# Head norms with tokens on the partitions: where the sums of squares of seven heads are taken

## The chip, the cores and the metric

The kernel runs on one core of one Trainium2 chip. The metric is device time in microseconds. The time before is 871.75 us, the median of three runs (871.43 to 872.48).

## The reference, cut to what matters

The program is one layer of a hybrid encoder over 512 tokens of width 1024. Two of its three branches end each head with an RMS norm over the head's 128 channels: four heads of a gated recurrence and four heads of differential attention.

```python
def rms_norm(x, g):
    xf = x.astype(jnp.float32)
    y = xf * lax.rsqrt(jnp.mean(xf * xf, axis=-1, keepdims=True) + NORM_EPS)
    return (y * g).astype(x.dtype)

# diff_attention: a = softmax(s0) - lam * softmax(s1), per head and block of 128 queries
    o = o.swapaxes(0, 1).reshape(B, S, ATT_HEADS, ATT_V_DIM)
    o = rms_norm(o, gain) * (1.0 - lambda_init)

# hgrn2_mixer: a forward and a backward scan, per head
    o = rms_norm((o_f + o_b).astype(q.dtype), gain).reshape(B, S, REC_WIDTH)
    return o * jax.nn.silu(g)
```

The kernel divides the attention weights by the first softmax's sum only after the product with the values. With Z that sum, the head's unnormalised output u stands for o = u / Z, and the norm becomes u * r with r = (1/Z) * (mean(u^2) * (1/Z)^2 + eps)^(-1/2). In the code 1/Z is `rr`, then `r0`.

## The kernel before, in words

Activations are kept transposed: channels on the 128 partitions, the 512 tokens along the free axis, in four blocks of 128 tokens (`NB`). Projections are products of a high and a low part of both operands, three terms of eight matmuls with 512 columns each, written to the PSUM tiles `mm`. Weights arrive by DMA in `raw`, and ScalarE (`whi`) and VectorE (`wlo`) split them.

The program order on TensorE is fixed when the program is built. A small planner, `Pipe.run`, holds several Python generators: one for each head and one for the stream of projection jobs. It keeps a clock `pipe.t` that each matmul and transpose advances. A generator yields `("w", t, slack)`, which means that it need not come back before t us later (and may be put off by slack), or `("e", name, t)`, which makes it wait for a mark. When no head is due, the stream issues products, in steps of two. So a head's small pieces sit between products, and the numbers in the yields decide how many products lie between. The other engines' order is made by a scheduler that simulates the program.

The recurrence head (`rec_scan`) ends with four groups of matmuls into a PSUM tile `rc`: the values `v_rec` as stationary operand against the scores `pt`, plus the states `st` against the gated queries `kq`, all 128x128 f32. The result has channels on the partitions. The attention head (`att_head`) multiplies the values (`va`) with the transposed probabilities (`aT`) into `rc`, also with channels on the partitions.

Both then call `head_norm`. ScalarE squares the tile into `sqo` and copies it into `og`, times the per-channel gain. TensorE multiplies each 128x128 block of `sqo` with a column of 1/128, which gives the mean square of 128 tokens on 128 partitions, one column of `tp` per block; with f32 operands each such matmul shows as two in the trace. VectorE adds eps (`ms`; in attention it multiplies by `r0` twice as well, `mo`), POOL takes the power -1/2 (`rso`), and in attention VectorE multiplies by `r0` again. TensorE then transposes each column of `rso`, broadcast to 128 columns, so that r lies along the free axis on all partitions. VectorE multiplies `og` with it (in the recurrence after it has multiplied with the gate `sg`), and the result is split in `y_arena` or `y_hi` and `y_lo`.

In the trace, line 96 is the helper that records matmuls and line 104 the one that records transposes. `hT` is the projection's activation, `s` a tile of exponentials, `co` the softmax coefficient that POOL computes from `zz`.

Of the kernel before, what the change touches and what calls it, by code (L numbers as in the profile page):

```python
# [11 lines left out]
F32 = mybir.dt.float32  # L12
F32R = mybir.dt.float32r
U8 = mybir.dt.uint8
AF = mybir.ActivationFunctionType
ALU = mybir.AluOpType
PSUM = bass.MemoryType.PSUM

P = 128
S = 512  # L20
D = 1024
NB = S // P
KT = D // P
HEADS = 4
FFN = 2816
FT = FFN // P
EPS = 1e-6
# [55 lines left out]
def encoder_kernel(ctx: ExitStack, tc: tile.TileContext, x, norm1_g, w_in, pool_w, pool_scale,  # L83
# [3 lines left out]
    nc = tc.nc  # L87
# [7 lines left out]
    def mm(out_, lhsT, rhs, start, stop, chain=False):  # L95
        i = nc.tensor.matmul(out_, lhsT=lhsT, rhs=rhs, start=start, stop=stop, skip_group_check=chain)  # L96
        tc.keep_in_program_order(i)
        n = 1
        for d in rhs.shape[1:]:
            n *= d  # L100
        pipe.t += max(0.107, n * 0.0004167 + 0.002) if rhs.dtype == F32R else max(0.216, n * 0.001667 + 0.004)

    def transpose(out_, in_, idn):
        tc.keep_in_program_order(nc.tensor.transpose(out_, in_, idn))  # L104
        pipe.t += 0.108
# [11 lines left out]
    small = ctx.enter_context(pool("small", 5))  # L117
    psum = ctx.enter_context(pool("psum", 3, space=PSUM))

    def bank(name, shape=(P, 512)):  # L120
        return psum.tile(list(shape), F32, name=name, bufs=2 if name == "tp" else 3)
# [7 lines left out]
    ident = const.tile([P, P], F32, name="ident")  # L129
    make_identity(nc, ident)  # L130
    fixed = const.tile([P, 2], F32, name="fixed")
    onesD, minus1 = fixed[:, 0:1], fixed[:, 1:2]
    nc.vector.memset(onesD, 1.0 / P)
    nc.vector.memset(minus1, -1.0)
    mhalf = const.tile([P, 8], F32, name="mhalf")
    nc.vector.memset(mhalf, -0.5)
# [2 lines left out]
    gain_a = const.tile([P, 1], F32, name="gain_a")  # L139
# [4 lines left out]
    gain_r = vcol[:, 13:14]  # L144

    def pow_mhalf(dst, src):
        return nc.gpsimd.tensor_tensor(out=dst, in0=src, in1=mhalf[:, :src.shape[1]], op=ALU.pow).ins  # L147

    def rsqrt_eps(dst, mean):

        ms = small.tile([P, 8], F32, name="ms")[:, :mean.shape[1]]
        eng = nc.vector if mean.space == PSUM else nc.gpsimd
        eng.tensor_scalar(out=ms, in0=mean, scalar1=1.0, scalar2=EPS, op0=ALU.mult, op1=ALU.add)  # L153
        return pow_mhalf(dst, ms)

    LAST, FF = {}, {}
# [434 lines left out]
    ps = bank("mm")  # L591
# [13 lines left out]
    ps = bank("mm")  # L605
# [17 lines left out]
    last = first_split((on_act, on_dve))  # L623
    for h, b, where in ((h0, 0, ("tp", "tp")), (h1, 1, ("rc", "mm"))):
        for half in range(2):
            with behind(last):
                on_act = rows_T(h, hT, b, half, None, where[half])
            last = on_act, LAST["hT_lo"]
# [4 lines left out]
    last = on_act, on_dve  # L633
    h2, on_dve, on_act = norm_rows(xt[2], g_b, xw, last)
    h3, on_dve, on_act = norm_rows(xt[3], g_b, xw, (on_act, on_dve))
    last = first_split((on_act, on_dve))
# [52 lines left out]
        nc.vector.tensor_copy(out=masks, in_=maskf)  # L689
    st0.close()  # L690

    def head_norm(o_ps, tmp, gain, r0=None, bufs=2, slack=0.0):


        og = tmp.tile([P, S], F32, name="og", bufs=bufs)
        sq = tmp.tile([P, S], F32, name="sqo", bufs=bufs)
        nc.scalar.activation(out=sq, in_=o_ps, func=AF.Square)
        nc.scalar.activation(out=og, in_=o_ps, func=AF.Copy, scale=gain)
        yield ("w", 1.3, slack)
        sp = bank("tp")  # L700
        for b in range(NB):
            mm(sp[:, b:b + 1], sq[:, b * P:(b + 1) * P], onesD, True, True)
        r = small.tile([P, NB], F32, name="rso")
        if r0 is None:
            rsqrt_eps(r, sp[:, 0:NB])
        else:
            m = small.tile([P, NB], F32, name="mo")
            nc.vector.tensor_tensor(out=m, in0=sp[:, 0:NB], in1=r0, op=ALU.mult)
            nc.vector.tensor_tensor(out=m, in0=m, in1=r0, op=ALU.mult)
            nc.vector.tensor_scalar(out=m, in0=m, scalar1=EPS, scalar2=None, op0=ALU.add)  # L710
            pow_mhalf(r, m)
            nc.vector.tensor_tensor(out=r, in0=r, in1=r0, op=ALU.mult)
        yield ("w", 3.55, slack)
        rb = bank("tp")
        for b in range(NB):
            transpose(rb[:, b * P:(b + 1) * P], r[:, b:b + 1].to_broadcast([P, P]), ident)
        return og, rb
# [124 lines left out]
    fronts, sgs = {}, {}  # L842
# [70 lines left out]
    def rec_scan(h):  # L913
# [85 lines left out]
                nc.vector.scalar_tensor_tensor(out=own, in0=st[:, 3 * d + prev, :], scalar=total, in1=ps[:, j, :],  # L999
                                               op0=ALU.mult, op1=ALU.add)  # L1000
        yield ("w", 2.4 if h < 3 else 1.6, slack)
        ps = bank("rc")
        for b in range(NB):
            o = ps[:, b * P:(b + 1) * P]
            mm(o, vs[b], pt[:, b, :], True, False)
            for d in range(2):
                if 0 <= b - 1 + 2 * d < NB:
                    j = b - 1 if d == 0 else b
                    mm(o, st[:, 3 * d + j, :], kq[:, 1 - d, b * P:(b + 1) * P], False, b == (0 if d else 3) or d == 1)
        mark(f"O{h}")  # L1010
        og, rbp = yield from head_norm(ps, rt, gain_r, slack=slack)
        yield ("e", f"G{h}", 0.0)
        nc.vector.tensor_tensor(out=og, in0=og, in1=sgs.pop(h), op=ALU.mult)
        nc.vector.tensor_tensor(out=og, in0=og, in1=rbp, op=ALU.mult)
        nc.scalar.copy(out=y_rec[0][:, h, :], in_=og)
        nc.vector.tensor_tensor(out=y_rec[1][:, h, :], in0=og, in1=y_rec[0][:, h, :].bitcast(F32), op=ALU.subtract)

# [72 lines left out]
    def att_head(h):  # L1090
# [64 lines left out]
                mm(ps, a[:, k, es], r[:, k, :], i == 0 and k == 0, i == 2 and k == NB - 1)  # L1155
            yield
        mark(f"PV{h}")
        og, rbp = yield from head_norm(ps, at, gain_a, rr, 1, 6.0 if h < HEADS - 1 else 0.0)
        mark(f"AN{h}")
        nc.vector.tensor_tensor(out=og, in0=og, in1=rbp, op=ALU.mult)  # L1160
        nc.scalar.copy(out=y_attn[0][:, h, :], in_=og)
        nc.vector.tensor_tensor(out=y_attn[1][:, h, :], in0=og, in1=y_attn[0][:, h, :].bitcast(F32),
                                op=ALU.subtract)
# [733 lines left out]
```

## Time and profile before

| | before |
|---|---|
| median of three runs | 871.75 us (871.43 to 872.48) |
| profiled execution, its own time | 871.81 us |
| its span | 870.0 us |
| granted TensorE clock | 0.999 |
| busy: TensorE, VectorE, ScalarE, POOL | 862.4, 659.2, 448.7, 37.1 us |
| sums of squares by matmul (`tp<-fixed,sqo`) | 64 matmul records, from 124.5 to 331.7 us |
| broadcast transposes (`tp<-ident,rso`) | 32, from 130.0 to 334.5 us |

Times in views are microseconds from the start of the span, and the duration of one instruction is in nanoseconds where a group's mean is shown. The busy time of a group of matmuls is the union of their overlapping spans, so the distance from one start to the next is a better measure of what an instruction takes from TensorE.

### The profile page before, as it was taken

To read this page: it belongs to the slowest core of one execution; us is meant where nothing else is said; L and a number is where in the kernel's file an instruction comes from. 1 tells how busy PE (TensorE), PEld (TensorE's weight loads), DVE (VectorE), ACT (ScalarE), POOL (GpSimd) and SP (SyncE) were. 2 spreads that over 40 slices of the span, in tenths; PEclk is the share of its full clock that TensorE was granted. 3 is DMA by queue.
4 is the path that set the end of the run, shared out by engine and by line. 5 is a ranking of instruction groups with operands and counts; after the bars stand their busy time and mean duration, and the time that the engine had idled before them with its cause. 6 is when DMAs were issued, how large, how long until landed. Compare 5 with 4: busy or idle time off the path is not lost.

```text
span 870.0 us, 14113 instructions
## 1 busy us (share of the span) xinstructions
PE 862.4 (99%) x5713; PEld 786.1 (90%) x5713; DVE 659.2 (76%) x979; ACT 448.7 (52%) x721; POOL 37.1 (4%) x83
## 2 busy tenths in 40 slices
PE   9999999999999999999999999999999999999997
PEld 8989998888988888899999998999999999988886
DVE  6779644845757888987776756988888888847996
ACT  6644343435757664563354425655555655533563
POOL 2000000000102220000000001000000000000001
PEclk9999999999999999999999999999999999999999
DMA  8330113024133321343332840344433433355002
GB/s 245 98 122 25 50 49 121 25 74 151 43 95 90 90 68 49 97 146 98 97 98 97 288 124 1 85 112 128 114 98 108 136 98 99 121 194 192 2 1 98
DMA packets 115694, 87.54 MB, mean 101 GB/s; under 512 B 3862, under 2 KB 104748, under 8 KB 115628
## 3 DMA queue, kind: packets, MB, share of 16 engines
q1 hardware_dynamic: 115036, 85.57, 32.2%
q8 instruction: 45, 0.74, 0.4%
q10 hardware_dynamic: 592, 1.05, 0.3%
q14 instruction: 21, 0.17, 0.1%
HBM read 84.52 MB, written 2.10 MB: 100 GB/s over the span
## 4 chain that ended last, share of the span: by engine, by line
PE 98%; issue 1%; DMA 0%; DVE 0%; POOL 0%; ACT 0%; POOLq 0%
PE mm L96 65%; PE rc L96 28%; PE tp L96 3%; PE tp L104 2%; DMA xin<-in_x_dram 0%; PE rc L104 0%; DVE hrow L502 0%; POOL rstd L147 0%; ACT silu L1479 0%; ACT x L1503 0%; DVE x L1472 0%; DVE x L1481 0%; PE mm L104 0%; POOLq L1892 0%; POOL ms L153 0%
## 5 line engine op out<-in xcount | busy, mean ns | idle before, releaser
L191 ACT CAST whi<-raw 128x1024 fp32r<-128x1024 f32 (+1 forms) x134 | 127.5, 959 | 140.7 <-PE mm L96 95.2
L192 DVE TENSOR_TENSOR wlo<-raw,whi 128x1024 fp32r<-128x1024 f32 (+1 forms) x134 | 147.8, 1106 | 50.9 <-ACT whi L191 41.3
L96 PE MATMUL mm<-hT_hi,whi 128*128 128x512 f32 (+1 forms) x344 | 81.3, 370 | 0.0
L96 PE MATMUL mm<-hT_hi,wlo 128*128 128x512 f32 (+1 forms) x344 | 80.0, 368 | 0.0
L96 PE MATMUL mm<-hT_lo,whi 128*128 128x512 f32 (+1 forms) x344 | 78.8, 367 | 0.0
L96 PEld LDWEIGHTS mm<-hT_hi,whi 128*128 128x128 f32 x344 | 59.2, 188 | 10.3 <-ACT hT_hi L515 0.2
L96 PEld LDWEIGHTS mm<-hT_lo,whi 128*128 128x128 f32 x344 | 59.1, 188 | 9.8
L96 PEld LDWEIGHTS mm<-hT_hi,wlo 128*128 128x128 f32 x344 | 58.8, 188 | 9.5
L318 DVE TENSOR_TENSOR slo<-sums,shi 128x1024 fp32r<-128x1024 f32 x54 | 65.7, 1217 | 0.0
L316 ACT CAST shi<-sums 128x1024 fp32r<-128x1024 f32 x54 | 56.8, 1052 | 4.1 <-DVE sums L280 3.3
L276 DVE TENSOR_TENSOR sums<-raw 128x1024 f32<-128x1024 f32 x27 | 32.9, 1218 | 1.2 <-DMA raw<-in_w_in_dram 1.2
L96 PE MATMUL mm<-y_arena,whi 128*128 128x512 f32 x128 | 32.7, 394 | 0.0
L96 PE MATMUL mm<-whi,y_arena 128*128 128x256 f32 (+1 forms) x192 | 32.1, 317 | 0.0
L96 PE MATMUL rc<-kq,kc 128*128 128x128 f32 x224 | 30.4, 284 | 0.0
L96 PEld LDWEIGHTS rc<-kq,kc 128*128 128x128 f32 x224 | 29.2, 191 | 1.1
L961 DVE TENSOR_TENSOR kq<-kq,pyr 128x256 f32<-128x256 f32 x48 | 18.2, 420 | 15.8 <-PE rc L96 15.8
L96 PEld LDWEIGHTS mm<-whi,y_arena 128*128 128x128 f32 x192 | 27.9, 189 | 2.6
L929 ACT COPY kc<-kq 128x512 f32<-128x512 f32 x28 | 18.6, 667 | 21.6 <-DVE kq L955 8.2
L1114 ACT ACTIVATE s<-s,mx 128x512 f32<-128x512 f32 x32 | 23.0, 719 | 10.9 <-DVE mx L1112 10.2
L96 PEld LDWEIGHTS mm<-y_arena,whi 128*128 128x128 f32 x128 | 23.7, 188 | 5.1
L1413 DVE TENSOR_TENSOR g<-mm,g 128x256 f32<-128x256 f32 x21 | 8.9, 424 | 23.9 <-PE mm L96 23.4
L96 PE MATMUL mm<-fhi,shi 128*128 128x256 f32 x168 | 25.9, 276 | 0.0
(409 smaller groups left out, 2053.5 us busy)
## 6 DMA issues: line engine op xcount, KB each, us to landing
raw<-in_w_in_dram SPq DMA_DIRECT2D x44, 512.0 KB, 4.2
raw<-in_w_ffn_in_dram SPq DMA_DIRECT2D x44, 512.0 KB, 4.1
raw<-in_w_in_dram SPq DMA_DIRECT2D x8, 1024.0 KB, 5.2
raw<-in_w_ffn_out_dram SPq DMA_DIRECT2D x7, 1024.0 KB, 4.8
raw<-in_w_out_dram SPq DMA_DIRECT2D x4, 1024.0 KB, 10.1
xin<-in_x_dram SPq DMA_DIRECT2D x4, 512.0 KB, 4.6
raw<-in_w_up_rec_dram SPq DMA_DIRECT2D x2, 1024.0 KB, 7.6
raw<-in_w_up_pool_dram SPq DMA_DIRECT2D x2, 1024.0 KB, 5.0
```

The lines of the kernel that those rows point to most:

```text
L96: i = nc.tensor.matmul(out_, lhsT=lhsT, rhs=rhs, start=start, stop=stop, skip_group_check=chain)
L104: tc.keep_in_program_order(nc.tensor.transpose(out_, in_, idn))
L191: LAST["whi"] = nc.scalar.copy(out=hi, in_=view).ins
L192: LAST["wlo"] = nc.vector.tensor_tensor(out=lo, in0=view, in1=hi.bitcast(F32), op=ALU.subtract).ins
L276: nc.vector.tensor_tensor(out=strided(sums, 0, [[2 * half, 2], [1, half]]), in0=strided(self.raw, 0, [[3 * half, 2], [1, half]]), in1=stri ...
L316: nc.scalar.copy(out=hi, in_=view)
L318: on_dve = nc.vector.tensor_tensor(out=lo, in0=view, in1=hi.bitcast(F32), op=ALU.subtract).ins
L929: nc.scalar.copy(out=strided(kc, 0, [[2 * n, S // (2 * n)], [n, 2], [1, n]]), in_=strided(kq, 2 * S, [[2 * n, S // (2 * n)], [S + n, 2], [ ...
L961: nc.vector.tensor_tensor(out=xv, in0=xv, in1=tv, op=ALU.mult)
L1114: nc.scalar.activation(out=s, in_=s, func=AF.Exp, scale=-1.0, bias=mx[:, c:c + 1], accum_out=zz[:, i, c:c + 1])
L1413: on_dve = nc.vector.tensor_tensor(out=c["g"], in0=c["x"], in1=c["g"], op=ALU.add).ins
```

## The change

Seven heads take their sums of squares along the free axis, from a tile with tokens on the partitions.

In the recurrence the two operands of every output matmul change places, so that the output has tokens on the partitions. ScalarE squares it, VectorE sums the squares along the free axis (`token_sums`, a `tensor_reduce`), VectorE scales by 1/128 and adds eps, POOL takes the power, and VectorE multiplies the copied output by r, broadcast along the channels. TensorE then transposes the four blocks of the normalised output. One VectorE operation multiplies by gain and gate.

In the first three attention heads ScalarE copies the output, TensorE transposes its four blocks, and `token_sums` works on the transposed tile in PSUM. The fourth attention head keeps the matmuls with a column, now of ones. In all four the small steps on 1/Z, sums and r are POOL's. The broadcast transposes of r stay in attention, and the gain moves into VectorE's last multiply. The small tiles of four columns share the name `mo`, which the pool already had.

The waits that the heads yield to the planner change: in the recurrence 1.3 and 3.55 become one of 4.6; in attention 1.3 and 3.55 become 1.2 and 4.8 (3.5 in the last head).

```diff
-    nc.vector.memset(onesD, 1.0 / P)
+    nc.vector.memset(ones, 1.0)
...
-    def rsqrt_eps(dst, mean):
+    def rsqrt_eps(dst, mean, n=1):
         ms = small.tile([P, 8], F32, name="ms")[:, :mean.shape[1]]
-        eng = nc.vector if mean.space == PSUM else nc.gpsimd
-        eng.tensor_scalar(out=ms, in0=mean, scalar1=1.0, scalar2=EPS, op0=ALU.mult, op1=ALU.add)
+        eng = nc.vector if mean.space == PSUM or n > 1 else nc.gpsimd
+        eng.tensor_scalar(out=ms, in0=mean, scalar1=1.0 / n, scalar2=EPS, op0=ALU.mult, op1=ALU.add)
         return pow_mhalf(dst, ms)
...
+    def token_sums(o, tmp, bufs=2):
+        sq = tmp.tile([P, NB, P], F32, name="sqo", bufs=bufs)
+        ss = small.tile([P, NB], F32, name="mo")
+        nc.scalar.activation(out=sq, in_=o, func=AF.Square)
+        nc.vector.tensor_reduce(out=ss, in_=sq, op=ALU.add, axis=mybir.AxisListType.X)
+        return ss
+
-    def head_norm(o_ps, tmp, gain, r0=None, bufs=2, slack=0.0):
+    def head_norm(o_ps, tmp, r0, wait, bufs=2, slack=0.0, last=False):
         og = tmp.tile([P, S], F32, name="og", bufs=bufs)
-        sq = tmp.tile([P, S], F32, name="sqo", bufs=bufs)
-        nc.scalar.activation(out=sq, in_=o_ps, func=AF.Square)
-        nc.scalar.activation(out=og, in_=o_ps, func=AF.Copy, scale=gain)
-        yield ("w", 1.3, slack)
-        sp = bank("tp")
+        if last:
+            sq = tmp.tile([P, S], F32, name="sqo", bufs=bufs)
+            nc.scalar.activation(out=sq, in_=o_ps, func=AF.Square)
+        nc.scalar.copy(out=og, in_=o_ps)
+        rr = small.tile([P, NB], F32, name="mo")
+        nc.gpsimd.tensor_tensor(out=rr, in0=r0, in1=r0, op=ALU.mult)
+        yield ("w", 1.2, slack)
+        turned = bank("tp", (P, NB, P))
         for b in range(NB):
-            mm(sp[:, b:b + 1], sq[:, b * P:(b + 1) * P], onesD, True, True)
+            bs = slice(b * P, (b + 1) * P)
+            if last:
+                mm(turned[:, 0, b:b + 1], sq[:, bs], ones, True, True)
+            else:
+                transpose(turned[:, b, :], og[:, bs], ident)
+        if last:
+            sums = small.tile([P, NB], F32, name="mo")
+            nc.vector.tensor_copy(out=sums, in_=turned[:, 0, 0:NB])
+        else:
+            sums = token_sums(turned, tmp, bufs)
+        m = small.tile([P, NB], F32, name="mo")
+        nc.gpsimd.tensor_tensor(out=m, in0=sums, in1=rr, op=ALU.mult)
+        nc.gpsimd.tensor_scalar(out=m, in0=m, scalar1=1.0 / P, scalar2=EPS, op0=ALU.mult, op1=ALU.add)
         r = small.tile([P, NB], F32, name="rso")
-        if r0 is None:
-            rsqrt_eps(r, sp[:, 0:NB])
-        else:
-            m = small.tile([P, NB], F32, name="mo")
-            nc.vector.tensor_tensor(out=m, in0=sp[:, 0:NB], in1=r0, op=ALU.mult)
-            nc.vector.tensor_tensor(out=m, in0=m, in1=r0, op=ALU.mult)
-            nc.vector.tensor_scalar(out=m, in0=m, scalar1=EPS, scalar2=None, op0=ALU.add)
-            pow_mhalf(r, m)
-            nc.vector.tensor_tensor(out=r, in0=r, in1=r0, op=ALU.mult)
-        yield ("w", 3.55, slack)
+        pow_mhalf(r, m)
+        nc.gpsimd.tensor_tensor(out=r, in0=r, in1=r0, op=ALU.mult)
+        yield ("w", wait, slack)
         rb = bank("tp")
...
-        ps = bank("rc")
+        ps = bank("rc", (P, NB, P))
         for b in range(NB):
-            o = ps[:, b * P:(b + 1) * P]
-            mm(o, vs[b], pt[:, b, :], True, False)
+            o = ps[:, b, :]
+            mm(o, pt[:, b, :], vs[b], True, False)
...
-                    mm(o, st[:, 3 * d + j, :], kq[:, 1 - d, b * P:(b + 1) * P], False, b == (0 if d else 3) or d == 1)
+                    mm(o, kq[:, 1 - d, b * P:(b + 1) * P], st[:, 3 * d + j, :], False, b == (0 if d else 3) or d == 1)
         mark(f"O{h}")
-        og, rbp = yield from head_norm(ps, rt, gain_r, slack=slack)
+        o = rt.tile([P, NB, P], F32, name="og")
+        sums = token_sums(ps, rt)
+        nc.scalar.copy(out=o, in_=ps)
+        r = small.tile([P, NB, 1], F32, name="rso")
+        rsqrt_eps(r[:, :, 0], sums, P)
+        nc.vector.tensor_tensor(out=o, in0=o, in1=r.to_broadcast([P, NB, P]), op=ALU.mult)
+        yield ("w", 4.6, slack)
+        turned = bank("tp")
+        for b in range(NB):
+            transpose(turned[:, b * P:(b + 1) * P], o[:, b, :], ident)
         yield ("e", f"G{h}", 0.0)
-        nc.vector.tensor_tensor(out=og, in0=og, in1=sgs.pop(h), op=ALU.mult)
-        nc.vector.tensor_tensor(out=og, in0=og, in1=rbp, op=ALU.mult)
+        og = sgs.pop(h)
+        nc.vector.scalar_tensor_tensor(out=og, in0=turned, scalar=gain_r, in1=og, op0=ALU.mult, op1=ALU.mult)
...
-        og, rbp = yield from head_norm(ps, at, gain_a, rr, 1, 6.0 if h < HEADS - 1 else 0.0)
+        og, rbp = yield from head_norm(ps, at, rr, 4.8 if h < HEADS - 1 else 3.5, 1, 6.0 if h < HEADS - 1 else 0.0, h == HEADS - 1)
         mark(f"AN{h}")
-        nc.vector.tensor_tensor(out=og, in0=og, in1=rbp, op=ALU.mult)
+        nc.vector.scalar_tensor_tensor(out=og, in0=og, scalar=gain_a, in1=rbp, op0=ALU.mult, op1=ALU.mult)
```

The planner puts the heads' pieces elsewhere between the products. On TensorE at the end of the fourth recurrence head, just after the head's output matmuls (`rc<-kq,st`, from here on `rc<-st,kq`), as a difference:

```order
 L96 MATMUL mm<-hT_lo,whi 128x512 x4
-L96 MATMUL mm<-hT_hi,wlo 128x512 x4
-L96 MATMUL tp<-fixed,sqo 128x1 x4
-L96 MATMUL mm<-hT_hi,wlo 128x512 x4
-L96 MATMUL mm<-hT_hi,whi 128x512 x8
+L96 MATMUL mm<-hT_hi,wlo 128x512 x8
+L96 MATMUL mm<-hT_hi,whi 128x512 x8
+L96 MATMUL mm<-hT_lo,whi 128x512 x2
+L104 MATMUL tp<-ident,og 128x128 x4
 L96 MATMUL mm<-hT_lo,whi 128x512 x6
-L104 MATMUL tp<-ident,rso 128x128 x4
-L96 MATMUL mm<-hT_lo,whi 128x512 x2
```

The four sums leave, and the one block of transposes that is left, now of `og`, stands behind 22 products instead of 26.

On TensorE in the attention, at the second head's norm, where the third head's scores and its transposes of `s` are already interleaved (numbers behind `s` tell tiles apart), before:

```order
L96 MATMUL mm<-hT_hi,whi 128x512 x4
L96 MATMUL tp<-fixed,sqo 128x1 x4
L96 MATMUL mm<-hT_hi,whi 128x512 x4
L104 MATMUL tp<-ident,s_2788 128x128 x4
L96 MATMUL mm<-hT_lo,whi 128x512 x8
```

and in the change:

```order
L96 MATMUL mm<-hT_hi,whi 128x512 x4
L104 MATMUL tp<-ident,og 128x128 x4
L96 MATMUL mm<-hT_hi,whi 128x512 x4
L96 MATMUL mm<-hT_lo,whi 128x512 x2
L104 MATMUL tp<-ident,s_2779 128x128 x4
L96 MATMUL mm<-hT_lo,whi 128x512 x6
```

The transposes of `og` take the place of the sums, and the next transposes of `s` come two products later.

On POOL at the same head, between two softmax coefficients, as it was and as it is:

```order
L1120 TENSOR_TENSOR co<-zz,nlam 128x1
L1121 TENSOR_TENSOR co<-zz,fixed 128x1
L147 TENSOR_TENSOR rso<-mo,mhalf 128x4
L1122 TENSOR_TENSOR co<-co 128x1
L1120 TENSOR_TENSOR co<-zz,nlam 128x1
```

```order
L1146 TENSOR_TENSOR co<-zz,nlam 128x1
L725 TENSOR_TENSOR mo<-mo 128x4
L726 TENSOR_SCALAR mo<-mo 128x4
L1147 TENSOR_TENSOR co<-zz,fixed 128x1
L147 TENSOR_TENSOR rso<-mo,mhalf 128x4
L1148 TENSOR_TENSOR co<-co 128x1
L729 TENSOR_TENSOR rso<-rso,rr 128x4
```

Two steps of the head's norm come in front of the coefficient's power, and one behind its last product.

More of the change, by code (lines that the diff above doesn't have):

```diff
@@ L131, in encoder_kernel @@
     fixed = const.tile([P, 2], F32, name="fixed")
-    onesD, minus1 = fixed[:, 0:1], fixed[:, 1:2]
-    nc.vector.memset(onesD, 1.0 / P)
+    ones, minus1 = fixed[:, 0:1], fixed[:, 1:2]
+    nc.vector.memset(ones, 1.0)
     nc.vector.memset(minus1, -1.0)
```

## The prediction

> **What bounds the kernel now.** I read the page first: busy shares, the clock row, the chain that ended last.
>
> ```profile
> span 870.0 us, 14113 instructions
> ...
> PE 862.4 (99%) x5713; PEld 786.1 (90%) x5713; DVE 659.2 (76%) x979; ACT 448.7 (52%) x721; POOL 37.1 (4%) x83
> ...
> PEclk9999999999999999999999999999999999999999
> ...
> PE 98%; issue 1%; DMA 0%; DVE 0%; POOL 0%; ACT 0%; POOLq 0%
> ```
>
> 98% of the chain is TensorE, at full granted clock throughout. A busy share of 99% could still hide waits, so the next view is the list of TensorE's waits, which has a single row, and after it the weight splits that feed TensorE.
>
> ```profile
> PE mm L96 <- POOL ident masks.py:199: 1.3, 1, 1.3
> ```
>
> ```profile
> L191 ACT CAST whi<-raw 128x1024 fp32r<-128x1024 f32 (+1 forms) x134 | 127.5, 959 | 140.7 <-PE mm L96 95.2
> ```
>
> TensorE waits once, 1.3 us at the start, and never again; ScalarE's split idles mostly because TensorE has not yet given a buffer back. So everything around the seven heads is paced by TensorE's program order: an instruction taken out of it shortens the span by its slot, and nothing that another engine does costs time until it makes TensorE wait. Thus the working has two halves: slots out and in, and the margin before each operand that TensorE will need.
>
> **The slots.** The last attention head shows sums, products and broadcast transposes in one place (start, duration, group):
>
> ```profile
> 329.64 1.53 PE L96 MATMUL mm<-hT_lo,whi 128*128 128x512 f32 x6
> 331.00 0.95 PE L96 MATMUL tp<-fixed,sqo 128*128 128x1 f32 x8
> 331.82 0.70 PE L96 MATMUL mm<-hT_lo,whi 128*128 128x512 f32 x2
> 332.36 2.01 PE L96 MATMUL mm<-hT_hi,wlo 128*128 128x512 f32 x8
> 334.21 0.60 PE L104 MATMUL tp<-ident,rso 128*128 128x128 f32 x4
> 334.57 2.09 PE L96 MATMUL mm<-hT_hi,whi 128*128 128x512 f32 x8
> 336.50 1.98 PE L96 MATMUL mm<-hT_lo,whi 128*128 128x512 f32 x8
> 338.31 1.98 PE L96 MATMUL mm<-hT_hi,wlo 128*128 128x512 f32 x8
> ```
>
> Durations overlap, so I take starts. Eight products alone take 338.31 - 336.50 = 1.81 us. Eight products around a sums block (four ones-matmuls, eight recorded passes) take 332.36 - 329.64 = 2.72: the block costs **0.91**, of which the start of its successor shows only 0.82. Four broadcast transposes and eight products take 336.50 - 334.21 = 2.29: **0.48**. The new attention transposes are of real data, like the softmax's; such a block stands beside the second attention head's norm:
>
> ```profile
> 285.37 0.95 PE L96 MATMUL tp<-fixed,sqo 128*128 128x1 f32 x8
> ...
> 287.20 0.60 PE L104 MATMUL tp<-ident,s 128*128 128x128 f32 x4
> ...
> 287.56 2.09 PE L96 MATMUL mm<-hT_lo,whi 128*128 128x512 f32 x8
> ...
> 289.49 0.40 PE L96 MATMUL rc<-k,q 128*128 128x512 f32 x1
> ...
> 293.59 0.60 PE L104 MATMUL tp<-ident,rso 128*128 128x128 f32 x4
> ```
>
> 289.49 - 287.20 - 1.81 = 0.48 again: real data costs no more than a broadcast.
>
> **The change part by part, on TensorE.** Removed: the sums of seven heads, 7 x 0.91 = 6.4 us. The last attention head keeps its own. Recurrence: four broadcast transposes per head go and four of the normalised output come, 0.48 for 0.48. The output matmuls swap stationary and moving operand, both 128x128 f32 before and after: nothing. Attention, three heads: four transposes each are added ahead of the sums and the broadcast ones stay, 3 x 0.48 = 1.4 us. Net 6.4 - 1.4 = **5.0 us less**; with one block beside another set of transposes, or read at the bare 0.90 and 0.47, it is 4.9. I use 4.9.
>
> By the Trainium skill, page "TensorE: Matmul & The Clock Gate", section "Part 4: PE-mode transpose", a 128x128 transpose takes about 275 ns in a kernel and doesn't count as busy for the clock. By that price twelve would cost 3.3 us. The duration agrees (272 in the row below); four in a row, though, occupy 0.48 here, and the clock row shows no loss around the transposes that are there already.
>
> **The other engines.** Prices from the grouped view:
>
> ```profile
> L96 PE MATMUL tp<-fixed,sqo 128*128 128x1 f32 x64 | 7.5, 241 | 0.0
> ...
> L104 PE MATMUL tp<-ident,s 128*128 128x128 f32 x64 | 9.6, 272 | 0.0
> ```
>
> ```profile
> L867 DVE TENSOR_SCALAR kq<-kq,om 128x512 f32<-128x512 f32 x8 | 3.8, 479 | 0.0
> L1014 DVE TENSOR_TENSOR og<-og,tp 128x512 f32<-128x512 f32 x4 | 2.7, 686 | 8.0 <-PE tp L104 8.0
> L1123 DVE SCALAR_TENSOR_TENSOR s<-s,co,s 128x512 f32<-128x512 f32 x16 | 12.0, 750 | 9.4 <-POOL co L1122 6.5 <-ACT whi L191 1.4 <-ACT aT_hi L1132 1.4
> L153 DVE TENSOR_SCALAR ms<-tp 128x4 f32<-128x4 f32 x4 | 0.6, 160 | 1.6 <-PE tp L96 1.4
> ```
>
> ```profile
> L147 POOL TENSOR_TENSOR rso<-ms,mhalf 128x4 f32<-128x4 f32 x4 | 4.0, 1010 | 176.8 <-DVE ms L153 176.8
> L153 POOL TENSOR_SCALAR ms<-ss 128x1 f32<-128x1 f32 x8 | 2.1, 261 | 213.2 <-ACT hrow L494 213.0
> ```
>
> Whoever sums along the free axis has to pay for it on VectorE. No free-axis reduction of this kind is in the trace. It reads 512 f32 a partition and writes four: at least the 0.48 of a one-input VectorE operation, at most the 0.75 of the dearest over the same elements. I take 0.69, the two-input row, since the cheap one is the only kind below it. A recurrence head then costs VectorE one reduction more, and one 0.75 operation for a 0.69: +0.75 us. An attention head trades four small operations (4 x 0.16) for one reduction: nothing. ScalarE keeps two passes per head; in attention the Square moves behind the transposes. All this lies beside products. The tightest stretch I found for VectorE is the third attention head:
>
> ```profile
> 300.00:320.00 20.00, 20.00 (x102) 16.66 (x100) 17.34 (x41) 12.18 (x27) 5.29 (x11) 1.00 0.37 119
> ```
>
> The fifth column is VectorE: 17.34 of 20 us busy, 2.7 spare. Without such cover the recurrence's extra work would cost 4 x 0.75 = 3 us.
>
> POOL takes over the attention's small steps: a square of 1/Z early, then product, scale, power and product. Nearest in operation is 0.26, and 1.01 is the power on the same shape, so a small step lies between; I take 0.26, because none of them is a power. The chain in POOL is 3 x 0.26 + 1.01 = 1.8 us.
>
> **The margins.** A head's result must be there when TensorE reaches its transposes. I followed the changed order against old times.
>
> Fourth recurrence head, the thinnest. Rows around it:
>
> ```profile
> 193.22 1.17 PE L96 MATMUL mm<-hT_lo,whi 128*128 128x512 f32 x4
> ...
> 200.16 0.60 PE L104 MATMUL tp<-ident,rso 128*128 128x128 f32 x4
> ```
>
> ```profile
> 197.22 1.23 DVE L192 TENSOR_TENSOR wlo<-raw,whi 128x1024 fp32r<-128x1024 f32 x1 [0.94 <-PE mm L96]
> ```
>
> ```profile
> 193.50 0.60 ACT L697 ACTIVATE sqo<-rc 128x512 f32<-128x512 f32 x1 [3.79 <-PE rc L96]
> ```
>
> 26 products and one sums block lie between 193.22 and 200.16: (6.94 - 0.91) / 26 = 0.232 each. The new order puts 22 ahead of the transposes: 193.22 + 5.10 = 198.32. The operand: Square to 194.10, reduction 194.8, small step 195.0, power about 196.1; but a weight split stands in front of the final multiply on VectorE. It waited for a product group that now ends 0.91 earlier: 196.31 to 197.54, then the multiply to 198.23. Margin 0.1. The same reckoning leaves about 1 us at the first two heads (the second also behind a weight split) and several at the third.
>
> Second attention head: its transposes take the slot at 285.37, the broadcast ones stay at 293.59. Between lie Square 0.6 (queued behind an exponential), reduction 0.69, POOL 1.8 and hops, say 5 us with queueing, of 8: margin over 2. Of what queues behind on POOL, the softmax's coefficient now follows the power; its own combine on VectorE, which the transposes ahead of 293.59 read, keeps about 1.5 us by my count. Last attention head: sums end at 331.95 and its transposes start at 334.21; copy 0.16, POOL 1.8 and some 0.3 for the hops between engines (an estimate) end at 334.2. Margin near zero. For these two places I add 0.15 us.
>
> Sum, against the profiled execution's own time, 871.81 (1.81 outside its span): 871.81 - 4.9 + 0.15 = 867.06. The median of the runs shown is 0.06 lower: **867.0 us**.
>
> **The rivals.**
>
> *Thin margins become waits.* Every place where the order left 0.1 costs some tenths, and the small POOL steps tend towards 1.01. For it: three small steps sit on the last head's path, which has no margin. Against: its price is bounded by rows. At 1.01 each the POOL chain grows 3 x 0.75 = 2.25 us: 2.1 at the last head and 0.75 beyond the margin of 1.5 at each of three others, 4.4 in all: 871.75 - 4.9 + 4.4 = 871.3, and half of it gives 869.1.
>
> *Transposes at full duration.* If the twelve don't overlap with their neighbours, they cost 12 x 0.272 = 3.3 instead of 1.4: 868.9. Against: both blocks above were measured at 0.48. The 275 ns that the Trainium skill's page "TensorE: Matmul & The Clock Gate" states would be this case.
>
> *Nothing is gained.* The sums fill time in which TensorE would otherwise wait for weights, so each slot turns into a wait: 871.75. For it: little. Against: weight splits wait for TensorE, and the wait list is empty.
>
> *Slower: POOL's queue.* The head's three POOL steps now stand before softmax coefficients, and these decide the next transposes. POOL's operations stretch at times:
>
> ```profile
> 266.38 1.61 POOL L1121 TENSOR_TENSOR co<-zz,fixed 128x1 f32<-128x1 f32 x1 [0.30 <-ACT s L1114]
> ```
>
> If three small steps took 1.61 each, the chain is 3 x 1.35 = 4.05 us later, 2.55 beyond the margin, 7.65 over three heads: 871.75 - 4.9 + 7.65 = 874.5. It decides from 1.5 + (4.9 + 1.7) / 3 = 3.7 us of delay a head. Against: one-element products in the same trace are mostly far shorter, and the coefficients' power, not a product, shows the 1.61.
>
> **How the numbers follow.** Forecast 0.73; transposes at full duration 0.04; half of the thin margins 0.10; nothing gained, or all margins dear, 0.08; slower 0.05. Differences within 0.2%, 1.7 us, are what a measurement of this kernel can't tell from no change. Forecast and the two cases at about 869 are faster: 0.87; same 0.08; slower 0.05. The range goes from 866.0 (6.4 - 1.3 = 5.1 saved, no wait, and 0.6 for the spread of runs) to 869.8, which takes in the two cases near 869.
>
> **What would show it.** Sums rows fall from x64 to x8, transposes of og appear x28, rso falls from x32 to x16. Starts around an og block in attention should differ by 0.48 more than products alone. The span should be about 865.2 with TensorE still near 99% and no new row among its waits; a row naming og (VectorE) or rso (POOL) as releaser is the first rival, POOL ahead of softmax transposes the last. A reduction over 0.75 us, or a clock below 1.00 between 108 and 340 us, would break the working.

## The result, and the profile after

The changed kernel takes 866.86 us (median of four runs, 866.03 to 867.27) where the kernel before, on the same chip, takes 871.79 (871.43 to 872.48): 4.9 us less, a ratio of 0.9941 with a 95% interval of 0.9924 to 0.9959. The forecast was 867.0. The time given for a kernel is the median of its executions at a granted clock of 0.997 or more; two executions of one later kernel, 1072.89 and 879.3 us at 0.75 and 0.95, are left out.

The profiled execution took 867.27 us of its own time. The lines of its page that answer to those of before (span, busy shares, granted clock in 40 slices, chain of waits):

```profile
span 865.5 us, 14040 instructions
...
PE 857.5 (99%) x5669; PEld 781.5 (90%) x5669; DVE 661.5 (76%) x971; ACT 448.5 (52%) x721; POOL 39.5 (5%) x99
...
PEclk9999999999999999999999999999999999999999
...
PE 96%; DMA 2%; ACT 1%; issue 0%; DVE 0%; POOL 0%; POOLq 0%
```

TensorE is busy for 4.9 us less, at the same clock, and is still nearly the whole chain; the 2% of DMA are looked at below. TensorE's list of waits (in us: total, times, longest):

```profile
PE mm L96 <- POOL ident masks.py:199: 1.3, 1, 1.3
PE mm L96 <- DVE y_arena L826: 0.3, 1, 0.3
PE mm L96 <- ACT hT_hi L515: 0.2, 1, 0.2
```

No row names `og`, `rso` or a softmax tile: at none of the seven heads does TensorE wait for the new work. The two small waits lie elsewhere: the 0.3 at 493.5 us, the 0.2 at 10.5 us. This list counts matmuls alone. The weight loads, which run beside them, have a list of their own, and there one row of the heads appears:

```profile
PEld tp L104 <- POOL rso L729: 0.3, 1, 0.3
```

It is the last attention head's, at 328.94. What it costs is read below.

The groups that the change touches, on TensorE, then VectorE, then POOL (count, busy us, mean ns):

```profile
L104 PE MATMUL tp<-ident,og 128*128 128x128 f32 x28 | 4.2, 272 | 0.0
L104 PE MATMUL tp<-ident,rso 128*128 128x128 f32 x16 | 2.4, 275 | 0.0
L96 PE MATMUL tp<-fixed,sqo 128*128 128x1 f32 x8 | 0.9, 240 | 0.0
```

```profile
L698 DVE TENSOR_REDUCE mo<-sqo 128x4 f32<-128x512 f32 x7 | 4.8, 682 | 6.1 <-ACT sqo L697 6.1
L1040 DVE SCALAR_TENSOR_TENSOR sg<-tp,vcol,sg 128x512 f32<-128x512 f32 x4 | 3.0, 750 | 1.5 <-PE tp L104 1.5
```

```profile
L147 POOL TENSOR_TENSOR rso<-mo,mhalf 128x4 f32<-128x4 f32 x4 | 4.5, 1134 | 0.3
...
L710 POOL TENSOR_TENSOR mo<-rr 128x4 f32<-128x4 f32 x4 | 1.7, 422 | 0.3 <-DVE rr L1173 0.3
L729 POOL TENSOR_TENSOR rso<-rso,rr 128x4 f32<-128x4 f32 x4 | 1.0, 242 | 0.2
L725 POOL TENSOR_TENSOR mo<-mo 128x4 f32<-128x4 f32 x4 | 0.8, 201 | 13.3 <-DVE mo L721 10.5 <-DVE mo L698 2.8
L726 POOL TENSOR_SCALAR mo<-mo 128x4 f32<-128x4 f32 x4 | 0.8, 194 | 0.3
```

The records are x8, x28 and x16, as forecast. The reduction over 512 elements takes 682 ns (0.69 was assumed, between 0.48 and 0.75), and POOL's steps on 128x4 take 0.19 to 0.24 on average (0.26 assumed), but 0.42 on average at line 710, which has a reason found below.

Where the time went can be read by laying the starts of the same matmuls of both traces beside each other. The changed kernel is ahead by 0.23 us at 121 us, before the first changed head; that is start-up. It is ahead by 3.83 behind the four recurrence heads (3.60 from the heads, 0.90 each), and by 4.3, 4.8 and 5.2 behind the first three attention heads. At 342 us it is 5.22 ahead, of which 4.99 come from the heads.

What a block of `og` transposes takes in attention can be read at the third head of the changed kernel:

```profile
305.69 1.08 PE L96 MATMUL mm<-y_arena,whi 128*128 128x512 f32 x4
306.61 0.60 PE L104 MATMUL tp<-ident,og 128*128 128x128 f32 x4
306.96 1.18 PE L96 MATMUL mm<-y_arena,whi 128*128 128x512 f32 x4
307.98 0.63 PE L96 MATMUL mm<-y_arena,wlo 128*128 128x512 f32 x2
```

Four products alone take 306.61 - 305.69 = 0.92 us, the block and four products 307.98 - 306.61 = 1.37: 0.45 for the block, where 0.48 was forecast.

The last attention head, whose sums stay:

```profile
325.74 0.95 PE L96 MATMUL tp<-fixed,sqo 128*128 128x1 f32 x8
326.55 0.70 PE L96 MATMUL mm<-hT_lo,whi 128*128 128x512 f32 x2
327.10 2.02 PE L96 MATMUL mm<-hT_hi,wlo 128*128 128x512 f32 x8
328.95 0.65 PE L104 MATMUL tp<-ident,rso 128*128 128x128 f32 x4
329.35 2.09 PE L96 MATMUL mm<-hT_hi,whi 128*128 128x512 f32 x8
```

From its sums to the products behind its broadcast transposes 3.61 us pass, against 334.57 - 331.00 = 3.57 before: the margin that the prediction put near zero cost 0.04. Later 0.5 us of the lead is lost near 494 us, in the output projection: a weight transfer lands there when the changed TensorE, which comes earlier, is already close behind, and VectorE's two weight splits delay a merged operand that TensorE then waits for (the wait of 0.3 above). At the end of the span 4.5 remain. How much is lost near 494 us goes with when the transfer lands. In three profiles of this kernel ScalarE, which waits for it, starts its split at 489.42, 489.20 and 488.81 us; against the kernel before, 0.54, 0.40 (a wait of 0.33 at a weight load, without a row among the matmuls) and nothing are lost, and the spans are 865.5, 865.1 and 864.1.

### The profile page after: what moved, and what is told of

Same layout as the page of the kernel before. It is cut to its first block, busy times and chain, and to the rows that moved or that the text cites. A ratio compares the mean times of both kernels' runs of the same rounds, so it can differ in the third digit from the quotient of the medians.

```text
span 865.5 us, 14040 instructions
## 1 busy us (share of the span) xinstructions
PE 857.5 (99%) x5669; PEld 781.5 (90%) x5669; DVE 661.5 (76%) x971; ACT 448.5 (52%) x721; POOL 39.5 (5%) x99
## 4 chain that ended last, share of the span: by engine, by line
PE 96%; DMA 2%; ACT 1%; issue 0%; DVE 0%; POOL 0%; POOLq 0%
PE mm L96 64%; PE rc L96 28%; PE tp L96 2%; PE tp L104 2%; DMA raw<-in_w_out_dram 2%; PE rc L104 1%; ACT hT_hi L515 0%; ACT whi L191 0%; DVE wlo L192 0%; ACT silu L1505 0%; ACT x L1529 0%; DVE x L1498 0%; DVE x L1507 0%; DVE y_arena L826 0%; PE mm L104 0%
```

## The experiments

Ratios are to the kernel before on the same chip, with 95% intervals.

### The change again, and its two halves

The changed kernel once more; its recurrence part with the attention heads as before; and its attention part with the recurrence heads as before. The core of the two edits against the changed kernel:

```diff
# recurrence alone: attention heads use the former head_norm
-        og, rbp = yield from head_norm(ps, at, rr, 4.8 if h < HEADS - 1 else 3.5, ...)
+        og, rbp = yield from head_norm(ps, at, gain_a, rr, 1, 6.0 if h < HEADS - 1 else 0.0)
# attention alone: recurrence heads use the former head_norm
-                mm(o, pt[:, b, :], vs[b], True, False)
+                mm(o, vs[b], pt[:, b, :], True, False)
...
+        og, rbp = yield from head_norm(ps, rt, gain_r, slack=slack)
```

> The changed kernel unaltered, as the yardstick of this series. Slots theory: 866.9 +- 0.5. Where the profile shows TensorE waiting for the last piece of the attention branch's merged output before the output projection (0.3 us there in the first profile, nothing before), the wait should vary with the landing of the output weights (some 13 us after issue), since nothing of the heads lies there.

> Only the recurrence part of the change; the attention heads keep the column matmuls, VectorE's small steps and the gain in ScalarE's copy. Slots theory: four sums blocks of 0.91 go, transposes one for one, so 871.8 - 3.6 = 868.2. Rival 'the swapped operands or VectorE's new work matter': anything clearly off 3.6.

> Only the attention part; the recurrence as before. Slots theory: three sums blocks go, three blocks of transposes come, 3 x (0.91 - 0.48) = 1.3, so 870.5. Rival 'transposes cost their full 0.272 each': 3 x 0.91 - 3.3 = 0.5 slower, 872.3. Rival 'the whole gain is in the attention': 866.9.

Measured: the change again 866.99 us (866.53 to 867.7), 0.9947 [0.9935, 0.9959]. The recurrence alone 867.54 (867.23 to 868.33), 0.9954 [0.994, 0.9967], 4.1 us less than before. Attention alone 870.52 (870.21 to 871.44), 0.9988 [0.9979, 0.9997], 1.1 less. The halves add up to 5.2 where both together give 4.6. Each difference of medians carries some tenths from the stage near 494 us, so the traces are the better measure up to 330 us: the recurrence alone is 3.7 us ahead behind its four heads, some 0.1 of it from start-up, and attention alone 1.45 behind its three (0.44, 0.99 and 1.45). The terms of the sum were 3.6 and 1.3.

### The last attention head changed too

```diff
-        og, rbp = yield from head_norm(ps, at, rr, 4.8 if h < HEADS - 1 else 3.5, 1, 6.0 if h < HEADS - 1 else 0.0, h == HEADS - 1)
+        og, rbp = yield from head_norm(ps, at, rr, 4.8, 1, 6.0 if h < HEADS - 1 else 0.0)
```

> The changed kernel, with the fourth attention head on the new path too (wait 4.8 as the others). Slots theory: one more sums block out and one block of transposes in, 0.43 less: 866.4, if the longer chain (Square and reduction, 1.1 us more) is covered by the products that the planner puts in. Rival 'nothing covers the last head': the 1.1 us shows as a wait, 867.6.

Measured: 867.95 us (867.32 to 868.08), 0.9955 [0.9943, 0.9968]: 0.96 more than the change on the same chip, not 0.43 less. TensorE's waits in this kernel have one new row:

```profile
PE tp L104 <- POOL rso L729: 1.4, 1, 1.4
```

It is the last head's factor: 1.43 of recorded idle time, against 0.43 expected from the slot, which makes +1.0 (by starts, 1.15 are lost at this head). The larger planner wait of 4.8 did not move the broadcast transposes: the same ten products lie between as with 3.5 (the last eight start at 326.99, the transposes at 330.44). Thus the same edit that gains some 0.46 at each of three heads loses about 1 at the fourth, where the chain of transposes, Square, reduction and POOL no longer fits in ten products.

### Spare work in the slots

A spare sums block (four matmuls with a column of ones), and in another kernel a spare block of four transposes, before each of the seven heads' `og` transposes. Their results are overwritten by the transposes that follow, so the output is the same.

```diff
+        if not last:
+            for b in range(NB):
+                spare(turned[:, b, 0:1], og[:, b * P:(b + 1) * P], ones)
...
+        for b in range(NB):
+            spare(turned[:, b * P:b * P + 1], o[:, b, :], ones)
```

> The changed kernel with four spare column matmuls per head (seven heads) put straight ahead of the transposes of og into the same PSUM bank, where the transposes overwrite them; the planner does not count them. Slots theory: 0.81 to 0.91 a block, 5.7 to 6.4 more, 872.6 to 873.3. Rival 'sums filled time in which TensorE would wait': clearly less than 5.

> The changed kernel with four spare transposes of og per head (seven heads) ahead of the real ones, overwritten by them; the planner does not count them. Slots theory: beside other transposes a block takes 0.43 to 0.48, 3.0 to 3.4 more, 870.1. Rival 'transposes cost their full 0.272 each': 28 x 0.272 = 7.6 more, 874.5.

Measured, against 866.99 for the change: with spare sums 873.8 us (872.8 to 874.54), 1.0024 [1.0014, 1.0035]; with spare transposes 869.87 (869.25 to 870.93), 0.9981 [0.9972, 0.999]. These kernels and the next two ran on another chip than the 866.99; the kernel before takes 871.54 us there and 871.63 here. No head's sums, factor or `og` is waited for longer than in the changed kernel. By the starts in the traces, each spare sums block costs 0.84 to 0.88 us, **0.85** on average, and each spare block of transposes **0.43**: 5.95 and 3.04 for the seven. That is a little under the prediction's 0.91 and 0.48, which were read between products; the expectation had 0.81 to 0.91 and 0.43 to 0.48 for blocks that stand ahead of other transposes. In both kernels another 0.25 are lost ahead of the third attention head, where a weight load waits for a cast of the softmax's turned tile:

```profile
301.32 0.76 PEld L96 LDWEIGHTS rc<-aT_hi,va_hi 128*128 128x128 f32 x4 [0.39 <-ACT aT_hi L1169]
```

With spare sums the median's 6.8 holds this and later losses as well; in the profiled execution 0.83 go at 565 us, at a wait of 0.6 for an operand of the last stages. The rival price of four times 0.272 would have been 7.6 us for the seven blocks. The Trainium skill, page "TensorE: Matmul & The Clock Gate", section "Part 4: PE-mode transpose", gives about 275 ns for a transpose; the group's mean is 272, but four in a row take 430 to 480 of TensorE's stream, not 1100.

### The margins: reduction twice, power twice

```diff
-        nc.vector.tensor_reduce(out=ss, in_=sq, op=ALU.add, axis=mybir.AxisListType.X)
+        for _ in range(2):
+            nc.vector.tensor_reduce(out=ss, in_=sq, op=ALU.add, axis=mybir.AxisListType.X)
# and, in another kernel, attention heads only
-        pow_mhalf(r, m)
+        for _ in range(2):
+            pow_mhalf(r, m)
```

> The changed kernel with each of the seven free-axis reductions done twice (0.69 us more on VectorE per head; the output is the same). Margins theory: only the fourth recurrence head has less than 0.69 to spare, so about 0.5 more, 867.4, with one wait of TensorE there. Rival 'VectorE is the bound around the heads': 7 x 0.69 = 4.8 more, 871.7.

> The changed kernel with the power of the four attention heads done twice (1.02 us more on POOL per head; the output is the same). Margins theory: the last head has next to no margin and waits 1.0 us, the other three keep over 1 us: 867.9. Rival 'POOL's queue decides the softmax': every head waits, 4 x 1.0 more, 870.9.

Measured: reduction twice 870.07 us (869.77 to 872.01), 0.9988 [0.9979, 0.9997]; power twice 869.81 (869.12 to 870.3), 0.9979 [0.997, 0.9987]. Both are about 3 us more than the change (866.99), far over the expectations of 867.4 and 867.9. TensorE's waits with the reduction twice, and then with the power twice:

```profile
PE tp L104 <- POOL rso L730: 2.2, 1, 2.2
PE mm L96 <- POOL ident masks.py:199: 1.3, 1, 1.3
PE tp L104 <- DVE og L1034: 0.7, 1, 0.7
```

```profile
PE tp L104 <- POOL rso L730: 2.8, 2, 1.4
```

Of these the 0.7 is at the second recurrence head and the 2.2 at the first attention head; the 2.8 are 1.4 at the first attention head and 1.4 at the last. By starts these heads lose 0.9 and 2.4, and 1.65 and 1.6. The fourth recurrence head, called the thinnest, does not wait with its reduction doubled. So the first attention head has next to no margin in the changed kernel, and the prediction did not name it. Its POOL rows, VectorE's weight split at that time and TensorE's transposes, in the changed kernel:

```profile
260.69 0.20 POOL L725 TENSOR_TENSOR mo<-mo 128x4 f32<-128x4 f32 x1 [1.77 <-DVE mo L698]
260.98 0.19 POOL L726 TENSOR_SCALAR mo<-mo 128x4 f32<-128x4 f32 x1
261.26 1.02 POOL L147 TENSOR_TENSOR rso<-mo,mhalf 128x4 f32<-128x4 f32 x1
262.24 1.16 POOL L1146 TENSOR_TENSOR co<-zz,nlam 128x1 f32<-128x1 f32 x1
263.35 0.20 POOL L729 TENSOR_TENSOR rso<-rso,rr 128x4 f32<-128x4 f32 x1
```

```profile
262.12 1.23 DVE L192 TENSOR_TENSOR wlo<-raw,whi 128x1024 fp32r<-128x1024 f32 x1 [0.30 <-ACT s L1140]
```

```profile
263.67 0.60 PE L104 MATMUL tp<-ident,rso 128*128 128x128 f32 x4
```

The factor is ready at 263.55 and read at 263.67: a margin of 0.12 us. The chain is long here because a softmax step (line 1146) stands in POOL's queue before the head's last product, and it takes 1.16 us, where the median of this step is 0.19. It starts inside VectorE's split and ends with it (263.40, the split at 263.35).

Why 0.69 us of extra reduction cost 2.2 at this head shows in VectorE's rows of that kernel:

```profile
260.99 0.68 DVE L699 TENSOR_REDUCE mo<-sqo 128x4 f32<-128x512 f32 x1
261.59 0.68 DVE L1139 CUSTOM_DVE_ANT_0 s<-strip,rc 128x512 f32<-128x512 f32 x1
...
262.80 0.68 DVE L699 TENSOR_REDUCE mo<-sqo 128x4 f32<-128x512 f32 x1
263.39 1.22 DVE L192 TENSOR_TENSOR wlo<-raw,whi 128x1024 fp32r<-128x1024 f32 x1
```

The second reduction comes behind two of the softmax's maximum passes, so the sums are there at 263.48, not 261.67: 1.8 us late for 0.69 us of work, and then POOL's first step runs into the split and takes 1.11. At the second recurrence head, too, the final multiply was put behind two other operations of 0.68 and comes 1.9 us later than in the changed kernel, where it ends at 131.12 for transposes at 132.06, a margin of 0.94.

### A shorter chain in POOL

The same factor with fewer steps: r = (sum/128 + eps Z^2)^(-1/2), with 1/128 in the Square's scale and eps Z^2 prepared early. Between sums and factor POOL has one addition and the power. Then this chain with the last head changed too (its transposes two products earlier), this chain with the power twice, and the change itself again.

```diff
-        nc.gpsimd.tensor_tensor(out=m, in0=sums, in1=rr, op=ALU.mult)
-        nc.gpsimd.tensor_scalar(out=m, in0=m, scalar1=1.0 / P, scalar2=EPS, op0=ALU.mult, op1=ALU.add)
+        nc.gpsimd.tensor_tensor(out=m, in0=sums, in1=rr, op=ALU.add)
         r = small.tile([P, NB], F32, name="rso")
         pow_mhalf(r, m)
-        nc.gpsimd.tensor_tensor(out=r, in0=r, in1=r0, op=ALU.mult)
```

> The changed kernel, with the same arithmetic in fewer POOL steps for the attention heads: (sum/128 + 1e-6-like constant times Z squared) to the power -1/2, with the 1/128 put into the Square's scale and the constant times Z squared prepared early. Between the sums and the finished factor POOL then has one addition and the power, where the changed kernel has product, scale, power, product. TensorE's order is unchanged. Margin theory: TensorE doesn't wait for this chain in the changed kernel, except 0.04 us at the last head, so a chain that is about 0.56 us shorter gains nothing: the time of the changed kernel (866.9 to 867.0) within 0.2, and no new wait. Rival (POOL's chain is on the path at every attention head): up to 4 x 0.56 = 2.2 less, 864.7.

> The short POOL chain, and the last attention head transposed as the other three, its four transposes two products earlier (0.46 us) than in the run that did it with the long chain. That run waited 1.43 us for the last head's factor. Margin theory: 0.56 us (two steps gone) + 0.34 (the stretch of the last product, gone with it) + 0.46 (earlier transposes) = 1.36 of the 1.43 are made up, so the wait is 0 to 0.2 and the slot of the sums (0.43 net) is gained: changed kernel - 0.43 + 0.1, about 866.6 (866.3 to 866.9). Rival (another engine or TensorE's queue holds the last head's transposes, not POOL's chain): 867.9 as with the long chain.

> The short POOL chain with the power computed twice: the sums-to-factor chain is about 1.02 - 0.56 = 0.46 us longer than in the changed kernel, where the doubled power in the long chain cost two waits of 1.4 us (869.8). Margin theory, with POOL's stretching seen in the traces (an operation of POOL that begins while VectorE's 1.2 us weight split runs ends with the split): at the first attention head both powers begin before the split does, the softmax step that was stretched now comes behind them, and the factor is there at about 263.1, 0.5 us before TensorE reads it: no wait. At the last head the second power ends at about 329.3 against a slot at 328.95: a wait of 0.3 to 0.5. Time: changed kernel + 0.4, about 867.4 (867.2 to 867.7). Rival (POOL's length counts, not where the queue is stretched): both waits shrink by 0.56 each, 869.8 - 1.1 = 868.7.

> The changed kernel as it is, on the same chip as the three runs with the short chain, so that tenths can be compared: 866.9 (866.6 to 867.2). All theories agree.

Measured on one chip: the change 866.17 us (865.93 to 866.6), 0.9938 [0.9926, 0.9949]; the short chain 866.72 (866.23 to 867.17), 0.9943 [0.9932, 0.9955]; the last head too 866.45 (866.19 to 866.63), 0.9942 [0.9929, 0.9954]; the power twice 867.96 (867.33 to 868.36, ten runs), a ratio of the medians of 0.9959.

The short chain gains nothing, as the margin theory says, and not the rival's 2.2 us. Its median is even 0.55 above the change's beside it, though the two intervals overlap. In the profiles it is 0.33 behind at 342 us. Of this 0.21 is lost not among the matmuls' own waits but at a weight load behind the first attention head. On ScalarE a weight split waits 0.22 for its transfer, the cast of the softmax's turned tile behind it starts at 270.00 and not at 269.62 as in the change's trace beside it, and TensorE's weight load waits for the cast:

```profile
268.28 1.05 ACT L191 CAST whi<-raw 128x1024 fp32r<-128x1024 f32 x1 [0.22 <-DMA raw<-in_w_in_dram]
```

```profile
270.64 0.76 PEld L96 LDWEIGHTS rc<-aT_hi,va_hi 128*128 128x128 f32 x4 [0.35 <-ACT aT_hi L1157]
```

The start-ups of the two differ by 0.17 as well, and the 0.04 of the last head is gained. Nothing ties the losses to the shorter chain: the same weight load waits 0.25 in the second profile of the change and 0.39 in the kernel with the last head changed too, both with the long chain.

With the last head changed too, the wait of 1.43 is gone, and beside the change's trace TensorE is ahead by 0.45 more behind the removed sums; but the factor arrives just as it is read (power until 328.54, transposes from 328.59), and 0.24 goes back there. So the net is 0.2. The medians don't show it (0.28 more than the change): in its trace the stage near 500 us runs at the slower of two paces (last section), 0.57 more than in the change's. It is not shown to beat the changed kernel.

The profile of the power twice with the short chain is of the execution of 1072.89 us, so that its times can't be compared; the order in it can, and at the first attention head both powers stand ahead of the softmax step, as the margin theory had it. The 1.8 more than the change agrees with the rival's 1.7 and not with the theory's 0.4. Against the short chain beside it, it is 1.24 more. From that kernel's rows a second power, 1.1 us later with its gap, would leave the first head 0.6 and make the last one wait 0.5 (an estimate: its power ends at 262.04 and 328.65, the transposes start at 263.73 and 329.25). Where the other 0.7 lie is open.

## Why the prediction was right, and where not

**Bound by TensorE's program order: right.** The span fell by what TensorE's slots give, and spare blocks that nobody needed cost their slots in full.

**The slots: right.** Recurrence 3.6 forecast, 3.60 by starts. Attention 1.3 forecast, 1.4 by starts. A sums block at 0.91 compares with 0.90 a head in the recurrence and 0.85 for the spare ones, a block of transposes at 0.48 with 0.45 and 0.43. The sum of 4.9 stands against 4.99 read at 342 us. Taking starts and not durations was what mattered: by durations twelve transposes would have cost 3.3 us, and the forecast would have been 868.9.

**VectorE and POOL: right in size.** Reduction 682 ns against 0.69; small POOL steps 0.19 to 0.24 against 0.26. POOL's product took longer only where VectorE held it up.

**The margins: right in sum, incomplete in place.** The 0.15 us was meant for the two places that the working left with next to no margin, the fourth recurrence head and the last attention head; they cost 0 and 0.04. At the fourth recurrence head these rows of VectorE and TensorE decide:

```profile
193.40 1.22 DVE L192 TENSOR_TENSOR wlo<-raw,whi 128x1024 fp32r<-128x1024 f32 x1 [1.28 <-PE mm L96]
194.54 0.68 DVE L1033 TENSOR_TENSOR og<-og,rso 128x512 f32<-128x512 f32 x1
```

```profile
195.41 0.60 PE L104 MATMUL tp<-ident,og 128*128 128x128 f32 x4
```

The multiply ends at 195.22 behind the split, as worked out, with 0.19 left against the 0.1 forecast. Since the split itself waits for TensorE, a longer reduction does not reach this margin. The step that failed is the list of margins in attention: it named the second and the last head, and left out the first, where 0.12 us is left. The chain POOL 1.8 us was right for the operations alone (260.69 to 262.28 for three of them), but a softmax step stretched to 1.16 stands inside it. In the time this did not show. But 0.7 us more on VectorE, or one more power on POOL, gave 870.07 and 869.81: more than the 869.1 of the rival in which half of the thin margins turn into waits. So that rival was nearer than its reckoning let it look, which charged each head's lateness at its own length.

**The rivals.** Transposes at full duration and the slots that turn into waits are excluded by the spare blocks. The slower case, POOL before the softmax coefficients, had as its evidence a POOL row of 1.61 us and "POOL's operations stretch at times". That stretch has a cause (last section), and in every case seen it ends with the VectorE operation that was running, 1.23 us at most here. Even the doubled power made no softmax transpose wait.

**Not foreseen:** what happens 150 us later. In the first profile half a microsecond was given back near 494 us, and three sets of runs put the gain at 4.9, 4.6 and 5.4 us. That the median of the first came within 0.2 us of the forecast is therefore in part luck; the 3.6 and 1.4 of the heads are not. The forecast also named a span of 865.2 without a new row among the waits; it is 865.5, with the two small rows, neither of them at a head.

## What to carry to other kernels

Where one engine's program order paces a stage, price a removed or added block by the distance between starts around it, with and without it, and then check for every operand the time from ready to read; the gain is the sum of slots as long as each of these margins stays positive. Look for the margins at every instance of a loop, since the same code had 3.3 us at one head and 0.12 at the next. A small addition on a side engine can cost three times its duration when it loses its turn in that engine's queue, so a margin below the length of one neighbouring operation may turn out to be none. And read the waits of weight loads as well as those of matmuls: waits of 0.25 to 0.39 us there put off the matmuls behind them by 0.1 to 0.4, without a row among the matmuls' waits.

## What the runs showed of the hardware

**POOL waits for VectorE's operations with two tensors in SBUF.** Between 100 and 345 us of the kernels before and after, 17 POOL operations start with more than 0.14 us left of such a VectorE operation. Each is longer than the shortest record of its kind, by the time that was left less 0.12 to 0.15 us: 1.16 for 0.19 (1.11 left), 1.09 for 0.20 (1.03 left), 1.48 for 1.02 (0.60 left), and the 1.61 of the prediction's slower case for 0.54 (1.21 left). No other POOL operation there is over 0.05 longer: not one that had started before the VectorE operation, and not one beside the reduction or beside an operation with one tensor in PSUM. This is the reason for the mean of 0.42 us at line 710, and for the last 0.34 of the wait when the last head is changed too. The Trainium skill says so on its page "SBUF — State Buffer", section "Who interferes with whom": a VectorE instruction with two SBUF inputs contends with a GpSimd instruction that reads SBUF, and the one that issues second blocks until the first is done. The traces agree where POOL comes second. Where the VectorE operation came second, four times in the same stretch of the two kernels with 0.15 to 0.76 us left of a POOL operation, it took its usual time (1.22 for a split at 0.76 left), so no run here shows VectorE held up. The prediction would have done well to weigh the first half.

**The same products at two paces.** In the output projection a group of 24 products of 128x256 takes 2.82 us in the first profile of the changed kernel and 2.72 in the third (that of its last set of runs), at a granted clock of 1.00 in both. The rows, first profile and then third:

```profile
498.22 2.05 PE L96 MATMUL mm<-whi,y_arena 128*128 128x256 f32 x16
500.10 1.10 PE L96 MATMUL mm<-wlo,y_arena 128*128 128x256 f32 x8
501.04 1.22 PE L96 MATMUL mm<-whi,y_arena 128*128 128x256 f32 x9
```

```profile
497.46 1.98 PE L96 MATMUL mm<-whi,y_arena 128*128 128x256 f32 x16
499.27 1.07 PE L96 MATMUL mm<-wlo,y_arena 128*128 128x256 f32 x8
500.18 1.98 PE L96 MATMUL mm<-whi,y_arena 128*128 128x256 f32 x16
```

This goes on for some 16 us and makes 0.57 us between these two executions of the same kernel, beside the 0.5 of the wait at 494 us. No wait is recorded for it, and the cause stays open. Each of the two moves this kernel's time by about half a microsecond, and that is why the last tenths here were read from starts in the traces and not from medians.
